# Where a mixer's streamed operands lie against its weights: the distance changed to 36 words

## The chip, the cores and the metric

The kernel runs on one core of a Trainium2 chip. The metric is the device time of one execution in microseconds; the kernel before takes 826.99 us (median of three runs, 826.88 to 827.64). TensorE (PE) multiplies. Each of its matrix products has two operands in SBUF: 128x128 *weights*, which a separate weight load (PEld) brings into the array, and a *moving* operand of up to 512 words for each partition, which is streamed past them. VectorE is DVE, ScalarE is ACT, GpSimd is POOL, SyncE is SP.

## What is computed

One encoder layer on 512 tokens of width 1024, in float32:

```python
x = x + 0.5 * swiglu(rms_norm(x, ffn1_norm), ffn1_w_gate, ffn1_w_up, ffn1_w_down)   # width 2752
h = rms_norm(x, mix_norm)
u = h @ w_in                       # 512 Fourier columns | q 8x64 | k 2x64 | v 2x64
f_out = fourier_mixer(u[..., :512])  # Re(DFT over positions and 128 channels), x4 groups, then a linear map + bias
a_out = gqa_attention(q, k, v)       # head norms, axial rotary, softmax over 512 keys
x = x + concat([f_out, a_out]) @ w_out
x = x + 0.5 * swiglu(rms_norm(x, ffn2_norm), ffn2_w_gate, ffn2_w_up, ffn2_w_down)
y = rms_norm(x, final_norm)
```

## The kernel before

The layer is computed transposed: tiles have features on the partitions and the 512 tokens along them. To keep float32 accuracy, an operand is split in a high part, rounded to the matrix format, and the low rest; a product is then three matrix products (high x high, high x low, low x high), all added in one PSUM bank (`product`, L179). Most 512-word moving operands are read through `turned` (L176), which takes groups of 4 words 16 words apart, 32 of them, and comes back for the next 4 words; the text calls these *strided*, the others *flat*. The results of a bank are moved out by DVE and ACT.

There are three stages. FFN1 (about 0 to 339 us of the profile) and FFN2 (490 to 825) stream gate, up and down weights from HBM by DMA, split them in ACT and DVE, and multiply on PE. Between them lies the mixer. In the mixer the order of all five engines is written out by hand in the string `ORDER`; each of its words is one operation. Its matrix products are:

- projections k, q0 to q3, v: `hh`/`hl` (normed x, high and low) move, weights `w_in` lie in ring slots. (L183)
- Fourier projections f0 to f3 (L1014, L1015, L1016, `fproject_ops`): here pieces of `hh`/`hl` are the weights, and `w_in` moves, flat, 256 words.
- scores (L1150, L1151, `score_ops`): queries in `part` are weights, keys `ks` move, strided.
- transposes of the probabilities `e` (L1176), then values (L1219, `attended_ops`): `vst` is the weights, the transposed probabilities `ph` and `pl` move, strided.
- the transform over positions (L1073, `position_ops`): `eh`/`el` are weights, the tables `pos` move flat, 256 or 258 words, and `both` strided.
- the transform over channels (L185 to L188, called by `channel_ops`): `mapw` is weights, the spectra `dh`, `dl` move, flat, 256 or 258 words.
- results y0 to y7 (L183, `output_ops`): `w_out` lies in ring slots and in `more`, and `part` (mixed output and attention) moves, strided; 8 x 8 x 3 = 192 products.

The change is about addresses, so here is how they come about. SBUF tiles of a pool lie one behind the other, in the order in which they are made. `room(pool, n)` makes an unused tile of n bytes that only shifts what follows. All large tiles have lengths that are multiples of 64 words plus a known rest, so that an operand's place can be told by its address in words modulo 64, and all pieces of an operand share it, save where the text says otherwise. The *distance* of a product is the place of the moving operand less that of the weights, modulo 64. The places before, from the order and sizes of the tiles:

| operand | place | | operand | place |
|---|---|---|---|---|
| ring slots, `more` (weights) | 48 | | `near`: `part`, `eh`, `el`, `vst` | 36 |
| `hh`, `hl`, old spectra in them | 36 | | `ks`, `both`, `ph`, `pl`, `e` | 24 |
| Fourier weights (`FURTHER`) | 20 | | `pos` pieces of 258 words | 24, 26, 28, 30 |
| `chan` | 48 | | `pos` pieces of 256 words | 32 |
| FFN `at` / `rt` | 36 / 32 | | last tokens' weights `tw` (`ASIDE`) | 24 |

So the distance is 52 in the results, scores, values, projections and the FFN's strided products, 48 in the Fourier projections and the FFN's flat ones, 52 to 60 in the position transform, and 0 in the channel transform. In the last 10 us, `by_tokens` (L521, products on L533) uses `at` as weights and `tw` as the moving operand, 384 words, strided: distance 52.

The tiles of the mixer lie where FFN1's `at`, `rt` and `sums` tiles were, and FFN2's lie there after them; the framework makes a tile's first writer wait for the last readers of what was there. FFN2's opening uses four slots of its activation tile as weight slots (`lent`, L554), which fall on mixer tiles that the results still read.

Of the kernel before, what the change touches and what calls it, by code (L numbers as in the profile page):

```python
# [7 lines left out]
F32R = mybir.dt.float32r  # L8
# [5 lines left out]
P = 128  # L14
S = 512
D = 1024
KD = D // P
# [4 lines left out]
HD = 64  # L22
EPS = 1e-6
WARM = 9
FURTHER = 36
FURTHER_IN = "f0", "f1", "f2", "f3"
ROOM = 64
FRONT, LOWER, NEAR = 16, -12, 4
ASIDE = 40
NS = 12  # L30

GROUPS1 = ((0, "t", 1, 2), range(3, 9), range(9, 15), range(15, 21))
# [53 lines left out]
def encoder(ctx, tc, A, out):  # L86
# [4 lines left out]
    whole = cp.tile([P, FRONT + NS * KD * P + 2 * ROOM], F32R, name="ring")  # L91
# [3 lines left out]
    def room(pool, n):  # L95


        pool.tile([P, n // 4], F32, name=f"room{len(rooms)}")
        rooms.append(n)
# [6 lines left out]
    def bank(name):  # L106
# [7 lines left out]
    hh, hl = (  # L114
        [whole[:, k * KD * P + o * S + NEAR : k * KD * P + (o + 1) * S + NEAR] for k in range(KD)] for o in range(2)
    )
# [9 lines left out]
    def lows(lo, src, hi):  # L126
        nc.vector.tensor_tensor(out=lo, in0=src, in1=asf(hi), op=ALU.subtract)  # L127
# [7 lines left out]
    def further(tile, i, rooms=0):  # L135
        o = i * KD * P + rooms * ROOM + FURTHER
        return tuple(tile[:, o + j * KD * P : o + (j + 1) * KD * P].rearrange("p (a b) -> p a b", b=P) for j in range(2))
# [38 lines left out]
    def turned(ap):  # L176
        return ap.rearrange("p (a b c) -> p b a c", b=4, c=4)

    def product(ps, whi, wlo, mhi, mlo, first, last, cut=False, turn=False):  # L179
        if turn:  # L180
            ps, mhi, mlo = turned(ps), turned(mhi), turned(mlo)
            for a, b in ((whi, mhi), (whi, mlo), (wlo, mhi)):
                nc.tensor.matmul(ps, a, b, start=first and b is mhi and a is whi, stop=last and a is wlo)  # L183
            return
        nc.tensor.matmul(ps, whi, mhi, start=first, stop=False)  # L185
        for t in parts_of(CUT[0]) if cut else (slice(0, ps.shape[-1]),):
            nc.tensor.matmul(ps[:, t], whi, mlo[:, t], start=False, stop=False)
        nc.tensor.matmul(ps, wlo, mhi, start=False, stop=last)  # L188
# [92 lines left out]
    def ffn(norm, after, wgu, wd, wdt, groups, opening, closing):  # L281
# [6 lines left out]
        with tc.tile_pool(name=f"act{n_}", bufs=1) as ap, tc.tile_pool(name=f"sums{n_}", bufs=2) as sp:  # L288
# [7 lines left out]
            def place(j):  # L296
# [5 lines left out]
            tw = [  # L302
                ring[:, 3 * i * KD * P + ASIDE : 3 * i * KD * P + ASIDE + PLACES * LAST * P]
                .rearrange("p (m c) -> p m c", c=LAST * P) for i in range(2)
# [441 lines left out]
    n2 = Norm(2)  # L746
    with tc.tile_pool(name="mix", bufs=1) as mp, tc.tile_pool(name="mixt", bufs=1) as mt:

        room(mp, 96)
        kst = [[mp.tile([P, S], F32R, name=f"ks{v}{o}") for o in range(2)] for v in range(2)]  # L750
        both = mp.tile([P, S], F32R, name="both")
        pos = mp.tile([P, 4 * 258 + 3 * 256], F32R, name="pos")
        near = mp.tile([P, 18 * S + 2 * NEAR], F32R, name="near")
        part = [near[:, NEAR + i * S : NEAR + (i + 1) * S] for i in range(16)]
        eh, el = ([[part[4 * n + 2 * h + i].rearrange("p (a b) -> p a b", a=2) for i in range(2)] for h in range(2)] for n in range(2))
        vst = near[:, NEAR + 16 * S : NEAR + 18 * S].rearrange("p (v c o e) -> p v c o e", v=2, c=4, o=2)
        room(mp, 32)
        more_tile = mp.tile([P, 2 * KD * P + ROOM], F32R, name="more")
        more = [slot_at(more_tile, i) for i in range(2)]
        plain.extend(more)  # L760
# [5 lines left out]
        sin = mp.tile([P, S], F32, name="sin")  # L766
        chan = mp.tile([P, 4, P], F32R, name="chan")

        coss = [[pos[:, (2 * p + i) * 258 : (2 * p + i + 1) * 258] for i in range(2)] for p in range(2)]
        sins = [[None, pos[:, 1032:1288]], [pos[:, 1288:1544], pos[:, 1544:1800]]]  # L770
        sc = mp.tile([P, 4, 10], F32, name="sc")


        ops = {}

        def op(name):
            def put(f):
                assert name not in ops, name
                ops[name] = f
                return f  # L780

            return put
# [4 lines left out]
        def bank_for(name, readers=1):  # L787
            held[name] = [spare.pop(0), readers]
            return held[name][0]

        def read(name):
            held[name][1] -= 1
            if not held[name][1]:
                spare.append(held.pop(name)[0])
# [248 lines left out]

        mh, ml = ([e[g // 2][g % 2].rearrange("p a b -> p (a b)") for g in range(4)] for e in (eh, el))
        mapw = [(hh[0], hl[0]), (hh[1], hl[1])]

        def fold_ops(t):


            @op(f"map{t}")  # L1050
            def _():
                banks[f"map{t}"] = bank_for(f"map{t}")
                whi, wlo = (w[:, :4, :].rearrange("p a b -> p (a b)") for w in ws["fw"])
                product(banks[f"map{t}"], chan[:, 2 * t, :], chan[:, 2 * t + 1, :], whi, wlo, True, True)

            op(f"map{t}.h")(lambda: nc.scalar.copy(mapw[t][0], banks[f"map{t}"]))

            @op(f"map{t}.l")
            def _():
                lows(mapw[t][1], banks[f"map{t}"], mapw[t][0])  # L1060
                read(f"map{t}")

        def position_ops(g):


            gs = slice(g % 2 * P, (g % 2 + 1) * P)
            dh, dl = hh[2 + g % 2], hl[2 + g % 2]
            name = f"d{g}"

            def add(w, m, t, order=lambda ps: ps):  # L1070
                ps, first = banks[name], not started
                started.append(t)
                nc.tensor.matmul(  # L1073
                    order(ps[:, t]), w, m, start=first, stop=len(started) == 12, skip_group_check=True
                )

            started = []

            def sums(o):
                if not started:  # L1080
                    banks[name] = bank_for(name, 1)
                for i in range(2):
                    h, l = (e[g // 2][i][:, o, gs] for e in (eh, el))
                    t, m = (slice(256, 512), sins) if o else (slice(0, 258), coss)
                    if o and i == 0:
                        add(h, turned(both), slice(0, S), turned)
                        add(l, turned(both), slice(0, S), turned)
                    else:
                        add(h, m[0][i], t)
                        add(l, m[0][i], t)  # L1090
                    add(h, m[1][i], t)

            op(f"{name}0")(lambda: sums(0))
            op(f"{name}1")(lambda: sums(1))
            op(f"{name}.h")(lambda: nc.scalar.copy(dh, banks[name]))

            @op(f"{name}.l")
            def _():
                lows(dl, banks[name], dh)
                read(name)  # L1100
# [2 lines left out]

        def channel_ops(g):
            gs = slice(g * P, (g + 1) * P)
            dh, dl = hh[2 + g % 2], hl[2 + g % 2]

            @op(f"c{g}.c")
            def _():
                banks[f"pc{g}"] = pc = bank_for(f"pc{g}")  # L1110
                product(pc[:, 0:258], mapw[0][0][:, gs], mapw[0][1][:, gs], dh[:, 0:258], dl[:, 0:258], True, True)

            @op(f"c{g}.s")
            def _():
                banks[f"ps{g}"] = psn = bank_for(f"ps{g}")
                product(psn[:, 0:256], mapw[1][0][:, gs], mapw[1][1][:, gs], dh[:, 256:512], dl[:, 256:512], True, True)

            @op(f"c{g}.q")
            def _():
                fos[g, 0] = mt.tile([P, 256], F32, tag="fq", name=f"fq{g}")  # L1120
                nc.scalar.copy(fos[g, 0], banks[f"ps{g}"][:, 0:256])
                read(f"ps{g}")

            @op(f"c{g}.o")
            def _():
                q, pc = fos[g, 0], banks[f"pc{g}"]
                fos[g, 1] = o = tp.tile([P, S], F32, tag="g", name=f"fo{g}")
                b = fb[:, g : g + 1]
                nc.vector.tensor_scalar(
                    out=o[:, 0:257:256], in0=pc[:, 0:257:256], scalar1=b, scalar2=None, op0=ALU.add  # L1130
                )
                for out, how in ((o[:, 1:256], ALU.add), (o[:, 257:512], ALU.subtract)):
                    nc.vector.scalar_tensor_tensor(out=out, in0=pc[:, 1:256], scalar=b, in1=q[:, 1:256], op0=ALU.add, op1=how)
                read(f"pc{g}")

            op(f"c{g}.h")(lambda: nc.scalar.copy(mh[g], fos[g, 1]))
            op(f"c{g}.l")(lambda: lows(ml[g], fos[g, 1], mh[g]))
# [429 lines left out]
```

## Time and profile before

| | us |
|---|---|
| median of three runs | 826.99 |
| the profiled execution, its own time | 827.06 |
| its span, first to last instruction | 824.8 |
| PE busy / weight load busy | 816.9 / 750.4 |
| DVE / ACT busy | 639.2 / 464.6 |

What lies outside the span is 827.06 - 824.8 = 2.26 us. A PE product's record includes its way through the array, so records of neighbours overlap: a product is longer in the record than the step from its start to the next one's. Where products follow each other, the pace is the length of a row of them divided by their count.

### The profile page before, as it was taken

To read this page: it belongs to the slowest core of one execution; us is meant where nothing else is said; L and a number is where in the kernel's file an instruction comes from. 1 tells how busy PE (TensorE), PEld (TensorE's weight loads), DVE (VectorE), ACT (ScalarE), POOL (GpSimd) and SP (SyncE) were. 2 spreads that over 40 slices of the span, in tenths; PEclk is the share of its full clock that TensorE was granted. 3 is DMA by queue.
4 is the path that set the end of the run, shared out by engine and by line. 5 is a ranking of instruction groups with operands and counts; after the bars stand their busy time and mean duration, and the time that the engine had idled before them with its cause. 6 is when DMAs were issued, how large, how long until landed. Compare 5 with 4: busy or idle time off the path is not lost.

```text
span 824.8 us, 13679 instructions
## 1 busy us (share of the span) xinstructions
PE 816.9 (99%) x5406; PEld 750.4 (91%) x5406; DVE 639.2 (78%) x1005; ACT 464.6 (56%) x778; POOL 30.7 (4%) x34
## 2 busy tenths in 40 slices
PE   9999999999999999999999999999999999999997
PEld 7889999899989998888999888899988999899986
DVE  7998896489756947699998488998955896479574
ACT  7764664167524645677786357556632674256462
POOL 0110000000000000221100000100000000000001
PEclk9999999999999999999999999999999999999999
DMA  7664322323242213522020224453232332422222
GB/s 256 180 145 173 122 91 77 122 103 141 78 140 102 64 55 115 184 93 77 26 77 27 82 97 116 119 163 123 90 122 94 128 116 63 138 103 97 69 77 103
DMA packets 31168, 89.58 MB, mean 109 GB/s; under 512 B 3712, under 2 KB 8832, under 8 KB 31104
## 3 DMA queue, kind: packets, MB, share of 16 engines
q1 hardware_dynamic: 27776, 82.61, 29.2%
q0 software_dynamic: 2608, 5.12, 3.4%
q8 instruction: 42, 0.69, 0.3%
q10 hardware_dynamic: 720, 0.98, 0.3%
q14 instruction: 22, 0.18, 0.1%
HBM read 84.24 MB, written 2.10 MB: 105 GB/s over the span
## 4 chain that ended last, share of the span: by engine, by line
PE 92%; DVE 5%; issue 1%; ACT 0%; DMA 0%; POOLq 0%; POOL 0%; DVEq 0%; ACTq 0%
PE dn L183 25%; PE r L419 23%; PE q L419 12%; PE gu L183 8%; PE mix L183 7%; PE p L419 6%; PE gu L708 3%; PE mix L1219 1%; PE mix L1176 1%; DVE mx L1156 1%; PE mix L1073 1%; DVE pl L127 1%; PE mix L1015 1%; PE mix L1016 1%; PE mix L1014 1%
## 5 line engine op out<-in xcount | busy, mean ns | idle before, releaser
L419 PE MATMUL r<-rt,ring 128*128 128x256 f32 x1686 | 209.2, 276 | 0.0
L183 PE MATMUL dn<-at,ring 128*128 128x512 f32 x900 | 203.3, 381 | 0.5 <-DVE ring L127 0.4
L419 PEld LDWEIGHTS r<-rt,ring 128*128 128x128 f32 x1686 | 200.3, 188 | 0.8
L183 PEld LDWEIGHTS dn<-at,ring 128*128 128x128 f32 x900 | 168.0, 188 | 29.8 <-DVE ring L127 1.6
L419 PE MATMUL q<-rt,ring 128*128 128x256 f32 x840 | 106.6, 276 | 0.0
L127 DVE TENSOR_TENSOR ring<-s,ring 128x1024 fp32r<-128x1024 f32 x70 | 85.4, 1220 | 24.1 <-ACT ring L378 20.8
L419 PEld LDWEIGHTS q<-rt,ring 128*128 128x128 f32 x840 | 100.4, 188 | 0.0
L543 DVE SCALAR_TENSOR_TENSOR gx<-dn,gx 128x512 f32<-128x512 f32 x61 | 41.9, 688 | 67.6 <-PE dn L183 67.6
L378 ACT CAST ring<-s 128x1024 fp32r<-128x1024 f32 x70 | 73.5, 1050 | 28.0 <-PE p L419 13.7
L169 ACT CAST ring<-raw_dn 128x768 fp32r<-128x768 f32 (+3 forms) x58 | 45.2, 783 | 71.3 <-PE dn L183 62.1
L127 DVE TENSOR_TENSOR ring<-raw_dn,ring 128x768 fp32r<-128x768 f32 (+3 forms) x58 | 51.5, 891 | 5.6 <-PE r L419 4.4
L419 PE MATMUL p<-rt,ring 128*128 128x256 f32 x420 | 53.3, 276 | 0.0
L127 DVE TENSOR_TENSOR ring<-raw_g,ring 128x1024 fp32r<-128x1024 f32 x35 | 42.7, 1219 | 11.1 <-PE p L419 10.2
L419 PEld LDWEIGHTS p<-rt,ring 128*128 128x128 f32 x420 | 50.2, 188 | 0.0
L183 PE MATMUL gu<-ring 128*128 128x512 f32 x216 | 48.9, 381 | 0.0
L183 PEld LDWEIGHTS gu<-ring 128*128 128x128 f32 x216 | 40.4, 188 | 6.9
L378 ACT CAST ring<-raw_g 128x1024 fp32r<-128x1024 f32 x35 | 36.8, 1051 | 16.0 <-DMA raw_g<-in_wgu 8.8
L427 ACT COPY p<-r 128x256 f32<-128x256 f32 x35 | 12.9, 370 | 46.7 <-PE r L419 46.3
L451 ACT ACTIVATE g<-g 128x512 f32<-128x512 f32 x35 | 22.2, 633 | 23.4 <-DVE g L450 23.1
L387 ACT CAST ring<-raw_u 128x512 fp32r<-128x512 f32 x35 | 21.8, 624 | 16.6 <-PE q L419 16.0
L255 POOL TENSOR_TENSOR r<-ms,mhalf 128x4 f32<-128x4 f32 (+1 forms) x4 | 4.3, 1072 | 659.5 <-DVE ms L248 659.5
L464 DVE TENSOR_TENSOR u<-g,u 128x512 f32<-128x512 f32 x35 | 24.0, 685 | 6.1 <-ACT u L463 6.0
(271 smaller groups left out, 1323.1 us busy)
## 6 DMA issues: line engine op xcount, KB each, us to landing
raw_g<-in_wgu SPq DMA_DIRECT2D x35, 512.0 KB, 3.6
raw_u<-in_wgu SPq DMA_DIRECT2D x35, 512.0 KB, 4.3
raw_dn<-in_wd SPq DMA_DIRECT2D x40, 384.0 KB, 3.1
raw_gu<-in_wgu SPq DMA_DIRECT2D x12, 512.0 KB, 3.5
raw_o<-in_wo SPq DMA_DIRECT2D x8, 512.0 KB, 3.5
raw_dn<-in_wd SPq DMA_DIRECT2D x8, 448.0 KB, 3.4
raw_wq<-in_wins SPq DMA_DIRECT2D x4, 512.0 KB, 5.1
raw_f<-in_winf SPq DMA_DIRECT2D x4, 512.0 KB, 4.1
```

Of the source, the lines that this page charges most:

```text
L127: nc.vector.tensor_tensor(out=lo, in0=src, in1=asf(hi), op=ALU.subtract)
L169: nc.scalar.copy(hi[:, :n, :], raw[:, :n, :])
L183: nc.tensor.matmul(ps, a, b, start=first and b is mhi and a is whi, stop=last and a is wlo)
L378: nc.scalar.copy(hi, src)
L387: nc.scalar.copy(hi, src)
L419: nc.tensor.matmul(ps[:, t], a[:, ks], b[:, i, t], start=first and i == 0 and o == 0, stop=i == KH - 1 and o == 2, skip_group_check=not first,
L427: nc.scalar.copy(t, ps)
L451: nc.scalar.activation(b["g"], b["g"], AF.Silu)
L464: nc.vector.tensor_tensor(out=u, in0=b["g"], in1=u, op=ALU.mult)
L543: nc.vector.scalar_tensor_tensor(out=x[d][:, t], in0=ps[:, t], scalar=0.5, in1=x[d][:, t], op0=ALU.mult, op1=ALU.add)
L708: nc.tensor.matmul(turned(pss[c]), w[:, k % 2, c], turned(m[k]), start=k == 0 and m is hh and w is hi, stop=k == KD - 1 and w is lo,)
L1014: nc.tensor.matmul(ps, hh[k][:, cs], whi[:, a, :], start=k == 0, stop=False)
```

## The change

Six sets of places move; the number, order and shapes of the instructions stay. `near` becomes the first large tile of the mixer's pool and starts at place 20 (`STEP` = 4 words after its base at 16). `more`, `cos`, `sin` and `chan` follow, `more` and `chan` again at place 48. Then 32 bytes of room put `ks`, `both` and `pos` on place 56; a last room puts the pool of `e`, `ph` and `pl` on place 56 too, 128 bytes further than before. `FURTHER` = 24 puts the moving Fourier weights on place 8, `ASIDE` = 24 does so for the last tokens' weights, and `spectra` is a new set of views of the ring tile, 36 words behind the old ones, on place 8. The distances become 36 in results, scores, values, Fourier projections, channel transform and `by_tokens`; 36, 38, 40, 42 and 44 for `pos`, 36 for `both`. Projections and the FFN's other products keep theirs, and so does the product of `chan` with the linear map (distance 0, flat, 512 words). The new spectra reach 36 words into `hl[2]`, `hh[3]`, `hl[3]` and `hh[4]`.

```diff
-FURTHER = 36
+FURTHER = 24
...
-FRONT, LOWER, NEAR = 16, -12, 4
-ASIDE = 40
+FRONT, LOWER, NEAR, STEP = 16, -12, 4, 4
+ASIDE, ASIDE_D = 24, 36
...
+        room(mp, 64)
+        near = mp.tile([P, 18 * S + 2 * STEP], F32R, name="near")
+        part = [near[:, STEP + i * S : STEP + (i + 1) * S] for i in range(16)]
...
+        vst = near[:, STEP + 16 * S : STEP + 18 * S].rearrange("p (v c o e) -> p v c o e", v=2, c=4, o=2)
         room(mp, 96)
+        more_tile = mp.tile([P, 2 * KD * P + ROOM], F32R, name="more")
...
+        cos = mp.tile([P, S], F32, name="cos")
+        sin = mp.tile([P, S], F32, name="sin")
+        chan = mp.tile([P, 4, P], F32R, name="chan")
+
+        room(mp, 32)
         kst = [[mp.tile([P, S], F32R, name=f"ks{v}{o}") for o in range(2)] for v in range(2)]
         both = mp.tile([P, S], F32R, name="both")
         pos = mp.tile([P, 4 * 258 + 3 * 256], F32R, name="pos")
-        near = mp.tile([P, 18 * S + 2 * NEAR], F32R, name="near")
...
-        room(mp, 32)
-        more_tile = mp.tile([P, 2 * KD * P + ROOM], F32R, name="more")
...
         sc = mp.tile([P, 4, 10], F32, name="sc")
+        room(mp, 64)
...
+        spectra = [
+            [whole[:, o : o + S] for o in ((2 + i) * KD * P + j * S + NEAR + ASIDE_D for j in range(2))] for i in range(2)
+        ]
...
-            dh, dl = hh[2 + g % 2], hl[2 + g % 2]
+            dh, dl = spectra[g % 2]
```

The last replacement stands in `position_ops` and in `channel_ops`.

More of the change, by code (lines that the diff above doesn't have):

```diff
@@ L747, in encoder @@
     with tc.tile_pool(name="mix", bufs=1) as mp, tc.tile_pool(name="mixt", bufs=1) as mt:
-        room(mp, 96)
-        kst = [[mp.tile([P, S], F32R, name=f"ks{v}{o}") for o in range(2)] for v in range(2)]
-        both = mp.tile([P, S], F32R, name="both")
-        pos = mp.tile([P, 4 * 258 + 3 * 256], F32R, name="pos")
-        near = mp.tile([P, 18 * S + 2 * NEAR], F32R, name="near")
-        part = [near[:, NEAR + i * S : NEAR + (i + 1) * S] for i in range(16)]
-        eh, el = ([[part[4 * n + 2 * h + i].rearrange("p (a b) -> p a b", a=2) for i in range(2)] for h in range(2)] for n in range(2))
-        vst = near[:, NEAR + 16 * S : NEAR + 18 * S].rearrange("p (v c o e) -> p v c o e", v=2, c=4, o=2)
-        room(mp, 32)
+        room(mp, 64)
+        near = mp.tile([P, 18 * S + 2 * STEP], F32R, name="near")
+        part = [near[:, STEP + i * S : STEP + (i + 1) * S] for i in range(16)]
+        eh, el = ([[part[4 * n + 2 * h + i].rearrange("p (a b) -> p a b", a=2) for i in range(2)] for h in range(2)] for n in range(2))
+        vst = near[:, STEP + 16 * S : STEP + 18 * S].rearrange("p (v c o e) -> p v c o e", v=2, c=4, o=2)
+        room(mp, 96)
         more_tile = mp.tile([P, 2 * KD * P + ROOM], F32R, name="more")
@@ L767, in encoder @@
         chan = mp.tile([P, 4, P], F32R, name="chan")
+        room(mp, 32)
+        kst = [[mp.tile([P, S], F32R, name=f"ks{v}{o}") for o in range(2)] for v in range(2)]
+        both = mp.tile([P, S], F32R, name="both")
+        pos = mp.tile([P, 4 * 258 + 3 * 256], F32R, name="pos")
         coss = [[pos[:, (2 * p + i) * 258 : (2 * p + i + 1) * 258] for i in range(2)] for p in range(2)]
@@ L1105, in channel_ops @@
             gs = slice(g * P, (g + 1) * P)
-            dh, dl = hh[2 + g % 2], hl[2 + g % 2]
+            dh, dl = spectra[g % 2]
             @op(f"c{g}.c")
```

## The prediction

> **What bounds the kernel now.** First the page: its opening, and the shares of the chain of work that ended last.
>
> ```profile
> span 824.8 us, 13679 instructions
> PE 816.9 (99%) x5406; PEld 750.4 (91%) x5406; DVE 639.2 (78%) x1005; ACT 464.6 (56%) x778; POOL 30.7 (4%) x34
> PE 92%; DVE 5%; issue 1%; ACT 0%; DMA 0%; POOLq 0%; POOL 0%; DVEq 0%; ACTq 0%
> ```
>
> PE is the bound, and a change of its pace is a change of the time, wherever the chain runs over PE. Next, the stretches of the mixer (busy times of PE, PEld, DVE, ACT, POOL, counts in brackets), and pieces of the chain there and in FFN2 (start, length, what).
>
> ```profile
> 350.00:393.00 43.00, 42.72 (x260) 37.65 (x259) 41.36 (x86) 32.81 (x65) 8.43 (x5) 1.00 0.27 86
> 393.00:450.00 57.00, 57.00 (x403) 52.73 (x402) 53.50 (x108) 43.57 (x90) 2.46 (x4) 1.00 0.13 47
> 450.00:490.00 40.00, 40.00 (x183) 34.10 (x182) 24.31 (x33) 16.64 (x25) 0.00 (x0) 1.00 0.23 79
> ```
>
> ```profile
> 385.58 0.62 DVE pl L127
> 387.44 0.69 DVE pl L127
> 389.53 0.61 DVE mx L1156
> 393.26 0.12 PE mix L1016
> 449.72 40.30 PE mix L183 x183
> 579.45 2.72 PE r L419 x24
> ```
>
> Until about 393 us the chain runs over DVE (maxima, low parts); from there PE is busy in 57.00 of 57.00 and 40.00 of 40.00 us, at a granted clock of 1.00. So the price of each distance counts from 393 on, and at the very end. The last two rows give the pace of an undisturbed stream: results 40.30 / 183 = 220.2 ns at distance 52, FFN2's flat products 2.72 / 24 = 113.3 ns at 48.
>
> Third, whether a distance costs anything now. Groups by form, before the bar the count, behind it busy time and mean record in ns:
>
> ```profile
> L419 PE MATMUL r<-rt,ring 128*128 128x256 f32 x1674 | 209.0, 276 | 0.0
> L183 PE MATMUL mix<-near,ring 128*128 128x512 f32 x120 | 28.1, 381 | 0.0
> L1015 PE MATMUL mix<-ring 128*128 128x256 f32 x48 | 13.3, 277 | 0.0
> L1016 PE MATMUL mix<-ring 128*128 128x256 f32 x48 | 13.3, 277 | 0.0
> L1151 PE MATMUL mix<-ks,near 128*128 128x512 f32 x32 | 12.3, 385 | 0.0
> L1219 PE MATMUL mix<-pl,near 128*128 128x512 f32 x32 | 12.2, 383 | 0.0
> L1073 PE MATMUL mix<-pos,near 128*128 128x256 f32 x16 | 2.5, 280 | 0.0
> L1073 PE MATMUL mix<-both,near 128*128 128x512 f32 x8 | 2.5, 388 | 0.0
> L188 PE MATMUL mix<-ring 128*128 128x258 f32 x4 | 1.1, 284 | 0.0
> L187 PE MATMUL mix<-ring 128*128 128x256 f32 x4 | 1.1, 280 | 0.0
> L187 PE MATMUL mix<-ring,chan 128*128 128x512 f32 x2 | 0.8, 394 | 0.0
> ```
>
> ```profile
> L1014 PE MATMUL mix<-ring x48: 275/275/367, 374.8 to 425.8; 128*128 128x256 f32 x48
> L1073 PE MATMUL mix<-pos,near x40: 275/282/369, 429.8 to 444.2; 128*128 128x258 f32 x24, 128*128 128x256 f32 x16
> L1219 PE MATMUL mix<-ph,near x32: 380/384/493, 373.8 to 448.0; 128*128 128x512 f32 x32
> L533 PE MATMUL last<-ring,at x42: 325/328/419, 809.6 to 818.3; 128*128 128x384 f32 x42
> ```
>
> (The second fence has least, median and longest record; in these groups pauses spoil the mean.) The floor of a record is 275 ns for a flat product of 256 words and 380 for a strided one of 512. The FFN and the results sit on it. The mixer's short stretches lie 2 to 8 ns above, and the product of `chan` with the linear map, at distance 0, is 14 ns above the strided floor. So a place does cost, though single nanoseconds.
>
> The Trainium skill says otherwise. On its page "TensorE: Matmul & The Clock Gate", Part 2, PE has two independent read ports of SBUF, and loading the next weights takes no read bandwidth from the running matmul; by that, the change is worth 0 and the time stays at 827.0. The rows disagree: 280 to 284 ns beside 276 for nearly the same length.
>
> **Which pair matters.** The timeline shows when weights are loaded:
>
> ```profile
> 484.37 5.25 PEld L183 LDWEIGHTS mix<-near,ring 128*128 128x128 f32 x24
> 484.59 5.44 PE L183 MATMUL mix<-near,ring 128*128 128x512 f32 x24
> 426.35 0.38 PE L1151 MATMUL mix<-ks,near 128*128 128x512 f32 x1
> 426.57 0.39 PE L185 MATMUL mix<-ring,chan 128*128 128x512 f32 x1
> 426.80 0.40 PE L187 MATMUL mix<-ring,chan 128*128 128x512 f32 x1
> 427.03 0.40 PE L188 MATMUL mix<-ring,chan 128*128 128x512 f32 x1
> ```
>
> The loads begin 0.22 us ahead of their products, which is one product. So what streams beside a moving operand is the *next* product's weights. In the third row keys (place 24) stream while `chan` (48) is loaded: distance 40, the nearest to 36 that a strided product has here, and the step to the next start is 0.22 us, the floor. The next two steps, at distance 0, are 0.23. I take 36 for strided streams as clean, like 40.
>
> For flat streams the nearest row is a single one. The Fourier product at 393.26 in the chain (place 20) ends its group and streams while the weights of a transpose (place 48) are loaded: distance 36, and its step is 0.12 us where undisturbed ones are 0.113. One sample, with weights of another kind; it is a warning, and one end of the range.
>
> **The change part by part.** It adds and removes no instruction, DMA or queue entry; it moves places. Counts from 393 us on (busy, count in brackets: L1014, L1151, L1219, L1073):
>
> ```profile
> 393.00:450.00 57.00, 12.48 (x45) 1.00 0.13 47
> 393.00:450.00 57.00, 5.76 (x15) 1.00 0.13 47
> 393.00:450.00 57.00, 13.45 (x48) 1.00 0.13 47
> 393.00:450.00 57.00, 7.64 (x48) 1.00 0.13 47
> ```
>
> What stands above the floor there, and so the most that can be won with the floor as it is:
>
> - Fourier projections, 3 x 45 = 135 products: 277 - 275 = 2 ns each, 0.27 us. Most of their records are on the floor (L1014's median is 275). 48 to 36: I take half, 0.13; ends +0.54 (135 x 4, all like the `pos` and channel rows at 6 above) and -0.27.
> - Scores, 2 x 15 = 30, by L1151's 385 - 380 = 5: 0.15 us. Values, 48, by 384 and 383: 3.5 ns, 0.17 us. But a score or a value is often followed by a transpose, whose weights `e` move to place 56 together with `ks`, `ph` and `pl`: that pair stays at distance 0. I take a quarter of 0.32, 0.08.
> - Position transform: 24 products of 258 words at 282 against some 276, 0.14; 16 at 280, 0.08; 8 strided at 388, 0.06. From 52 to 60 to 36 to 44: half of 0.28, 0.14.
> - Channel transform, 8 x 3 = 24 products, 280 to 284: 6 ns, 0.14 us. It leaves distance 0, the worst place that the rows show; two thirds, 0.09.
> - Results, 192 products: 0.2 ns above 220, nothing to win at the floor.
> - Last tokens, 42 products: median 328 against the least, 325; at most 0.13, taken as 0.
> - Scores, values and Fourier products ahead of 393: hidden by DVE, taken as 0. Were PE the path there too, the same prices on 34, 16 and 57 products would give 34 x 5 + 16 x 3.5 + 57 x 2 = 0.34 us.
>
> Sum 0.13 + 0.08 + 0.14 + 0.09 = 0.44 us, of at most 0.27 + 0.32 + 0.28 + 0.14 + 0.13 = 1.14.
>
> Two more steps are costed at nothing. The waits on reused places: FFN2's borrowed slots fall on later pieces of `part` than before, which the last steps of y7 read. The work that hides this is a copy in front of them:
>
> ```profile
> 489.85 1.05 ACT L169 CAST ring<-raw_gu 128x1024 fp32r<-128x1024 f32 x1 [2.47 <-PE mix L183]
> 490.80 1.04 ACT L169 CAST at<-raw_gu 128x1024 fp32r<-128x1024 f32 x1
> 502.11 5.44 PE L183 MATMUL gu<-ring,at 128*128 128x512 f32 x24
> ```
>
> ACT already waits for the end of the results at 489.85 for a ring slot, writes the borrowed slot (`at`) at 490.80, and the products that need it begin at 502.11; a microsecond of waiting would vanish in 10. The same two rows show a copy to two different places taking 1.05 and 1.04, so I give the moved tiles no price on ACT and DVE. The spectra's 36 words in `hl[2]`, `hh[3]`, `hl[3]` and `hh[4]` add readers and writers in the order of `ORDER`: the Fourier products that read them are issued before d00, and y3.h and y4.h, which write them again, come after c3. No new wait.
>
> The profiled execution's own time is 827.06, 0.07 above the median of 826.99: 827.06 - 0.44 = 826.6, and the same by the median to the tenth.
>
> **The rivals.**
>
> *The new distance collides, and the kernel is slower.* Place: the results above all, the one long stretch that is on the floor now and can only lose. If 36 is to strided streams what distance 0 is in the `chan` row, each pays 14 ns: 30 + 48 + 8 + 192 = 278 products, 3.9 us, less the 0.3 that scores, values and `both` pay already; the 42 last ones three quarters of it, 0.4; the Fourier products 0.5. Together 4.5: 831.6. It decides from 1.65 us (0.2%, about what a measurement of this kernel tells from no change), which is 5.3 ns on some 310 strided products: a pace of the results of 225.5. For it speaks that 36 appears nowhere in this trace but in the 0.12 us row; against it, the 0.22 us at distance 40.
>
> *The floor itself falls.* From 256 to 512 words the pace grows by 220.2 - 113.3 = 106.9 ns, so 220.2 - 2 x 106.9 = 6.4 ns of each product are not spent on words. If half of it is a collision that 52 and 48 merely leave small, 278 + 42 + 135 + 24 + 40 = 519 products win 3.2 ns, 1.7 us, and the 1.14 above as well: 824.2; with all 6.4 ns it would be 822.6. Against it: distances 40, 48 and 52 all end on the same floor, and so do flat and strided streams. The same page of the Trainium skill, under "Back-to-back issue gap", gives N / 2.4 + 2.5 ns for matmuls in a row, 215.8 for 512 words; an estimate by it would be 4.4 ns less per result and 0.8 us over 192. The 220.2 measured is above it.
>
> *Nothing happens.* A stream that is interrupted needs a few products to settle whatever the places are, as the Fourier group does at the distance at which FFN2 runs on the floor. Time 827.0.
>
> **How the numbers follow.** Small gain as summed, 826 to 827: 0.43. Nothing: 0.17. Collision: 0.26, of which 0.22 above 0.2%. Lower floor: 0.14. So faster by over 0.2%: 0.14, within: 0.43 + 0.17 + 0.04 = 0.64, slower: 0.22. The time is that of the first, 826.6, whose own range is 825.8 to 827.4. The range of 8 in 10 reaches to the middle of the lower floor, 824.2, and to two thirds of the collision, 830.0.
>
> **What would show it.** Right: results still at 220 ns in the chain, L187 and L188 in the channel transform near 276, `pos` nearer 276 than 282, Fourier means at 275 to 276, scores and values hardly changed. Wrong: a results piece longer than 40.30 for 183 products (collision), or shorter than 40.2 (lower floor), or a PE row with a DVE or ACT releaser after 393 us that is not there now.

## The result and the profile after

The changed kernel takes 828.34 us (median of 22 runs), the kernel before 826.98 beside it on the same chip: a ratio of 1.0015, 95% interval 1.0008 to 1.0022. It is slower, by 1.36 us; 826.6 was forecast. The profiled execution took 828.41, against 827.06 before, so its 1.35 us more can be followed through the trace. First the page's opening, then pieces of the chain (start, length, what).

```profile
span 826.1 us, 13679 instructions
PE 819.1 (99%) x5406; PEld 751.4 (91%) x5406; DVE 639.0 (77%) x1005; ACT 464.4 (56%) x778; POOL 30.7 (4%) x34
```

```profile
339.89 4.09 PE mix L183 x18
394.01 0.90 PE mix L1224 x4
450.67 40.70 PE mix L183 x183
```

The first two answer to these of the kernel before:

```profile
339.76 4.09 PE mix L183 x18
393.82 0.89 PE mix L1219 x4
```

PE has 2.2 us more of busy time and the weight load 1.0, DVE, ACT and POOL none. The mixer begins 0.13 us later, ahead of anything that the change touches (the opening of FFN1, whose length varies from run to run, see below). The value products that began at 393.82 begin at 394.01: beside the 0.13, less than 0.1 us is lost ahead of them. The results begin at 450.67 in place of 449.72: another 0.76 us are gone between 394 and 450. The results take 40.70 in place of 40.30 us for the same 183 products, 222.4 ns each in place of 220.2: 0.40 us. At the end of the results 0.95 + 0.40 = 1.35 us are lost, as much as in the whole execution; 0.13 of it is the opening's, so some 1.2 us are the change's.

Ahead of 394 us, the slower products are hidden because PE had time to spare behind DVE. In the changed kernel that spare time is used up earlier: from this piece on the chain runs over PE, where before it went back to DVE (378.62 to 379.36 on PE, then a maximum on DVE) and came to PE for good at 391.27.

```profile
378.76 0.49 PE mix L1155
```

Groups by form say which products it was (busy us, mean record in ns; L1016 to L1018 are the Fourier lines that were L1014 to L1016, L1224 the values, L1156 the scores, L1078 the position transform):

```profile
L183 PE MATMUL mix<-near,ring 128*128 128x512 f32 x120 | 28.3, 383 | 0.0
L183 PE MATMUL mix<-near,more 128*128 128x512 f32 x72 | 17.3, 383 | 0.0
L1016 PE MATMUL mix<-ring 128*128 128x256 f32 x48 | 13.7, 285 | 0.0
L1017 PE MATMUL mix<-ring 128*128 128x256 f32 x48 | 13.6, 284 | 0.0
L1018 PE MATMUL mix<-ring 128*128 128x256 f32 x48 | 13.6, 283 | 0.0
L1156 PE MATMUL mix<-ks,near 128*128 128x512 f32 x32 | 12.3, 385 | 0.0
L1224 PE MATMUL mix<-pl,near 128*128 128x512 f32 x32 | 12.2, 383 | 0.0
L533 PE MATMUL last<-ring,at 128*128 128x384 f32 x42 | 8.3, 340 | 0.0
L1078 PE MATMUL mix<-pos,near 128*128 128x256 f32 x16 | 2.5, 280 | 0.0
L1078 PE MATMUL mix<-both,near 128*128 128x512 f32 x8 | 2.4, 386 | 0.0
L187 PE MATMUL mix<-ring 128*128 128x258 f32 x4 | 1.1, 286 | 0.0
L187 PE MATMUL mix<-ring 128*128 128x256 f32 x4 | 1.1, 282 | 0.0
```

The three Fourier lines went from 281, 277 and 277 ns to 285, 284 and 283. The results went from 381 and 380 to 383, which is the 0.40. Scores, values, position and channel transform are where they were, within 4 ns. The median record of the second Fourier line (L1015 before, L1017 now) shows that it is not a few slow products: it was 275, the floor, and is 283.

```profile
L1015 PE MATMUL mix<-ring x48: 275/275/283, 374.9 to 425.9; 128*128 128x256 f32 x48
L1017 PE MATMUL mix<-ring x48: 277/283/289, 375.0 to 426.8; 128*128 128x256 f32 x48
```

What a product costs the path is not its record but the step from its start to the next one's. Added up in both traces, from the value products at 393.82 (394.01) on to the end of the results' 183, the steps show where the time went (all other products of this stretch change by 0.02 us together):

| products | forecast, us | change of their steps, us |
|---|---|---|
| Fourier, 132 | -0.13 | +0.59 (4.5 ns each) |
| scores and values, 78 | -0.08 | +0.15 |
| position and channel transforms, 72 | -0.23 | +0.02 |
| results, 183 | 0 | +0.39 |

So at 36 neither stream settles on its floor. What had to be found out: is it the distance, or the moved tiles; does the place of the moving operand alone do it; and which distances settle.

### The profile page after: what moved, and what is told of

It reads as the page before. It is cut to its first block, busy times and chain, and to the rows that moved or that the text cites. A ratio compares the mean times of both kernels' runs of the same rounds, so it can differ in the third digit from the quotient of the medians.

```text
span 826.1 us, 13679 instructions
## 1 busy us (share of the span) xinstructions
PE 819.1 (99%) x5406; PEld 751.4 (91%) x5406; DVE 639.0 (77%) x1005; ACT 464.4 (56%) x778; POOL 30.7 (4%) x34
## 4 chain that ended last, share of the span: by engine, by line
PE 93%; DVE 4%; issue 1%; DMA 1%; ACT 0%; POOLq 0%; POOL 0%; DVEq 0%; ACTq 0%
PE dn L183 25%; PE r L419 23%; PE q L419 12%; PE gu L183 7%; PE mix L183 7%; PE p L419 6%; PE gu L708 3%; PE mix L1224 2%; PE mix L1181 1%; PE mix L1017 1%; PE mix L1016 1%; PE mix L1018 1%; PE mix L1078 1%; DVE mx L1161 1%; PE mix L1155 1%
```

## The experiments

Theory D: the distance decides whether a stream of products settles on its floor. Rival L: the time is lost by the moved tiles and their neighbours, in no pair of places. Rival P: the place of the moving operand decides, not its distance.

Where a kernel is given without a ratio, its single time is not compared: the opening of FFN1 takes a varying time (18.20 us for its first 80 products in the changed kernel's profile, 19.80 in that of s3, before anything of the change runs). This is mostly no wait: the first products themselves are slower for a while. In s3 the median record of the products that start ahead of 9 us is 628 ns, in the kernel before it is 380. Groups and chain pieces are compared instead. For timed kernels the ratio to the kernel before on the same chip is given.

### Fourier alone (e1)

```diff
--- before
-FURTHER = 36
+FURTHER = 24
```

> The kernel before with the moving Fourier weights alone put 36 words from hh (FURTHER = 24); all other places as before. Theory D (the distance decides whether a stream of products settles on its floor, and 36 lets neither flat nor strided streams settle): L1014 to L1016 go from 277 to 283-285 ns as in the changed kernel, 135 products from 393 us on at 5 to 6 ns, so 0.7 to 0.8 us slower: 827.7 to 827.8; the results stay at 220.2 ns. Rival L (the moved tiles and their neighbours, not the pairs of places, cost the time): 827.0 and 277 ns. Rival P (the place of the moving operand itself, 8 in place of 20, decides): like D in this run.

Measured: 828.26 us beside 827.53, ratio 1.0009 (1.0000 to 1.0018), so 0.7 us. Groups and chain:

```profile
L1014 PE MATMUL mix<-ring 128*128 128x256 f32 x48 | 13.7, 286 | 0.0
L1015 PE MATMUL mix<-ring 128*128 128x256 f32 x48 | 13.6, 283 | 0.0
L1016 PE MATMUL mix<-ring 128*128 128x256 f32 x48 | 13.6, 284 | 0.0
450.65 40.30 PE mix L183 x183
```

One constant gives the whole Fourier loss, and the results begin at 450.65, as in the changed kernel, but stay at 40.30. By steps, the 132 Fourier products behind the first values cost 4.7 ns more each than before, 0.63 us; scores and values, whose places are the old ones here, cost 0.14 more, so that part does not come from their own places. Rival L does not hold for this part.

### All but Fourier (e2)

```diff
--- changed kernel
-FURTHER = 24
+FURTHER = 36
```

> The changed kernel with the moving Fourier weights alone put back to distance 48 (FURTHER = 36). Theory D: L1016 to L1018 return to 277 ns, the results stay at 222.4 ns; 0.7 to 0.8 us faster than the changed kernel, 827.5, still 0.5 above the kernel before. Rival L: 828.3, no gain. Rival P: as D.

Measured: 827.93 us beside 827.53, ratio 1.0008 (0.9999 to 1.0017). Relative to the kernel before, 0.4 us is left of the 1.36 by the medians, 0.7 by the ratio. Groups and chain:

```profile
L1016 PE MATMUL mix<-ring 128*128 128x256 f32 x48 | 13.5, 281 | 0.0
L1017 PE MATMUL mix<-ring 128*128 128x256 f32 x48 | 13.3, 277 | 0.0
L1018 PE MATMUL mix<-ring 128*128 128x256 f32 x48 | 13.3, 277 | 0.0
452.49 40.70 PE mix L183 x183
```

The Fourier groups are back at the means of before, the results stay at 40.70. By the medians the two halves, 0.7 and 0.4, add up to most of 1.36. The timed ratios alone would not separate them from noise; the groups do. (The late start of the results in this profile is the opening's, whose first 80 products took 20.17 us.)

### Distance or place (e3)

Here `hh` and `hl` move, and the Fourier operands that stream past them stay on place 20.

```diff
--- before
-FRONT, LOWER, NEAR = 16, -12, 4
+FRONT, LOWER, NEAR, HERE = 16, -12, 4, 16
...
-        [whole[:, k * KD * P + o * S + NEAR : k * KD * P + (o + 1) * S + NEAR] for k in range(KD)] for o in range(2)
+        [whole[:, k * KD * P + o * S + HERE : k * KD * P + (o + 1) * S + HERE] for k in range(KD)] for o in range(2)
```

> The kernel before with hh and hl on place 48 in place of 36. The moving Fourier weights stay on place 20, but their distance becomes 36 because their weights moved. Theory D: L1014 to L1016 at 283 to 285 ns as in the changed kernel. Rival P (the place of the moving operand decides): 277 ns, as place 20 is kept. Beside it: all strided products that stream hh or hl (gates, tails, projections, some 530) get distance 0; if that costs 14 ns each as in the one flat row of distance 0, the time is some 7 us longer, 834; if strided streams do not mind distance 0, 827.

Measured groups and chain:

```profile
L183 PE MATMUL gu<-ring 128*128 128x512 f32 x216 | 49.9, 386 | 0.0
L1014 PE MATMUL mix<-ring 128*128 128x256 f32 x48 | 13.6, 283 | 0.0
L1015 PE MATMUL mix<-ring 128*128 128x256 f32 x48 | 13.4, 280 | 0.0
L1016 PE MATMUL mix<-ring 128*128 128x256 f32 x48 | 13.4, 280 | 0.0
451.94 40.31 PE mix L183 x183
```

At distance 36 with the old place of the moving operand, the second and third Fourier line take 280 ns (277 at 48, 283 to 284 at 36 in the changed kernel). By steps, the 132 products cost 3.3 ns more each than before, against 4.5 in the changed kernel. Rival P, 277, is out, and so is the place of the weights alone, which e1 did not move; but D's 283 to 285 was not reached either, so the places themselves have some part beside the distance, and that part stays open. The gates now stream at distance 0 and pay 386 - 381 = 5 ns, not the 14 that I had carried over from the flat row at distance 0.

### Both undone (d1)

```diff
--- changed kernel
-FURTHER = 24
+FURTHER = 36
...
-FRONT, LOWER, NEAR, STEP = 16, -12, 4, 4
+FRONT, LOWER, NEAR, STEP = 16, -12, 4, 36
...
-        room(mp, 64)
-        near = mp.tile([P, 18 * S + 2 * STEP], F32R, name="near")
+        near = mp.tile([P, 18 * S + 40], F32R, name="near")
...
-        room(mp, 96)
+        room(mp, 32)
...
-        room(mp, 32)
+        room(mp, 96)
...
-        room(mp, 64)
```

> The changed kernel with both suspects undone: the Fourier products at 48 and, by near on place 36, the results at 52; scores and position transform stay at 36 and more, the channel transform and the last tokens at 36; the values fall to distance 20. Theory D: L1016 to L1018 at 277 ns, results 220.2 ns, and what is left of the change is worth 0.1 to 0.3 us: within 0.05% of the kernel before. Rival L (moved tiles cost something that is in no pair of places): still 0.5 to 1 us slower.

Measured: 828.0 us beside 827.37, ratio 1.0004 (0.9995 to 1.0013; the medians are 0.63 us apart, by the ratio it is 0.3); chain and groups:

```profile
L1015 PE MATMUL mix<-ring 128*128 128x256 f32 x48 | 13.3, 277 | 0.0
L1016 PE MATMUL mix<-ring 128*128 128x256 f32 x48 | 13.3, 277 | 0.0
450.08 40.26 PE mix L183 x183
```

With the two distances back, both groups are on their old pace, though all tiles lie as in the changed kernel's order. The results begin 0.36 us later than before: 0.12 of it is lost ahead of the first values, and 0.16 is in the steps of the values, which lie at distance 20 and have 386 ns in their `pl` products against 383. Behind the results the profile loses another 0.3 us in FFN2, which the changed kernel does not, and the cause of that is open. The interval reaches from no loss to 1.1 us, most of the change's, so the time of this run does not decide between D and L; its groups do, for the two that matter.

### Other distances (s1, s2, s3, s4)

Four kernels vary `FURTHER`, the place of `near` (by `STEP` and the rooms around it), `ASIDE` and `ASIDE_D` together; each group has its own distance. The edit shown is that of s1; the figures in its first line are `FURTHER`, `STEP` and `ASIDE` of each kernel.

```diff
--- changed kernel          s1: 4, 24, 28   s2: 20, 32, 8   s3: 40, 4, 20   s4: 28, 40, 36
-FURTHER = 24
+FURTHER = 4
...
-FRONT, LOWER, NEAR, STEP = 16, -12, 4, 4
-ASIDE, ASIDE_D = 24, 36
+FRONT, LOWER, NEAR, STEP = 16, -12, 4, 24
+ASIDE, ASIDE_D = 28, 48
...
-        room(mp, 64)
-        near = mp.tile([P, 18 * S + 2 * STEP], F32R, name="near")
+        near = mp.tile([P, 18 * S + 24], F32R, name="near")
```

> The changed kernel with other distances: Fourier 16 (flat), results 40 and last tokens 40 (strided), channel transform 48, scores and values 32, position transform 32 to 40. Theory D with the place in lines of 16 words (flat streams settle where the distance is a multiple of 16, as 48 is): Fourier at 275 to 277 ns. Theory D with every distance of its own: no forecast for 16. For strided streams the five steps seen at 40 forecast 220.2 ns for the results and 328 for the last tokens. Rival P gives no forecast for new places; that settled and unsettled values do not go with the distances would speak for it.

> Distances: Fourier 32 (flat), results 48 (strided), last tokens 20 (strided), channel transform 16, scores and values 24. Theory D with lines of 16 words for flat streams: 32 settles like 48 and 16, L1015 to L1017 at 277 to 278 ns after the first. For strided streams only 52 has settled so far: results at 222 to 226 ns.

> Distances: Fourier 52 (flat), results 20 (strided, 52 less 32), last tokens 32, channel transform 32, scores and values 52. Theory D with lines of 16 words: flat 52 is 4 off a multiple of 16, as 36 is: 283 to 285 ns. If strided streams repeat every 32 words, results at 20 take 220.2 ns as at 52; if they repeat every 64 words only, 222 to 226.

> Distances: Fourier 40 (flat), results 56 (strided, 4 words beside 52), last tokens 48, channel transform 52, scores and values 16. Theory D with lines of 16 words: flat 40 lies midway between multiples of 16: 281 to 285 ns. Results at 56: 220.2 if what settles is a range around 52, 222 to 226 if it is 52 alone.

The results' chain pieces, in the order s1, s2, s3, s4, and after them one Fourier line (the second of the three) of each:

```profile
450.27 41.40 PE mix L183 x183
```

```profile
453.06 41.47 PE mix L183 x183
```

```profile
452.63 42.06 PE mix L183 x183
```

```profile
450.69 41.48 PE mix L183 x183
```

```profile
L1016 PE MATMUL mix<-ring 128*128 128x256 f32 x48 | 13.3, 278 | 0.0
```

```profile
L1016 PE MATMUL mix<-ring 128*128 128x256 f32 x48 | 13.6, 283 | 0.0
```

```profile
L1016 PE MATMUL mix<-ring 128*128 128x256 f32 x48 | 13.6, 282 | 0.0
```

```profile
L1016 PE MATMUL mix<-ring 128*128 128x256 f32 x48 | 13.4, 280 | 0.0
```

Divided by 183 and put beside the others:

| results, strided: distance | 52 | 36 | 40 | 48 | 56 | 20 |
|---|---|---|---|---|---|---|
| us for 183 | 40.30 | 40.70 | 41.40 | 41.47 | 41.48 | 42.06 |
| ns each | 220.2 | 222.4 | 226.2 | 226.6 | 226.7 | 229.8 |

| Fourier, flat: distance | 48 | 16 | 40 | 52 | 32 | 36 |
|---|---|---|---|---|---|---|
| ns, second line's mean | 277 | 278 | 280 | 282 | 283 | 284 |

For strided streams 52 stands alone among the six; four words beside it, at 48 and 56, the product costs 6.4 and 6.5 ns more, and it does not repeat after 32 words (20 is the worst). 36 is the second best of those tried. For flat streams 48 and 16 settle and 32 does not, which refutes the rule of multiples of 16 that I had put into the expectations of s1 to s4; 16 and 48 fit a period of 32 words, and two points are no proof of it. (16 is not quite like 48: in s1 some groups stay on 276 ns, others alternate between 278 and 281 to their end.)

Two limits of these rows. Within each of them only the moving operand's place varies, with the weights on 48 in the results and on 36 in the Fourier products, so they do not tell distance from place; for flat streams e1 and e3 do, in part, and for strided ones no run here does. And the order of the results' row does not carry over to short groups: in s2 the last tokens stream at distance 20, the worst of the row, and their mean of 339 ns lies between the 338 of the kernel before and the 341 of e3, both at distance 52:

```profile
L533 PE MATMUL last<-ring,at 128*128 128x384 f32 x42 | 8.3, 339 | 0.0
```

Of the distances tried, those of the kernel before are the best for both streams, so nothing points to a version that beats both kernels.

## Why the prediction was wrong

**What bounds the kernel, and where a pace counts:** right in the main. PE carries the path from 393 us on, and the loss by the end of the results (1.35 us, 0.13 of it the opening's) is that of the time (1.36); what the Fourier products lose ahead of 393 is hidden but for less than 0.1 us. But the spare time that hides it is not fixed: in the changed kernel the chain is on PE from 378.76.

**"I take 36 for strided streams as clean, like 40":** wrong, and this is the step that failed for the results. The row it rested on is one product in a short stretch. In a row of 183, distance 40 costs 226.2 ns (s1), and still 13 of those 183 steps are 220 ns in the trace. A single step on the floor does not show that a stream stays there. The term "nothing to win at the floor" was 0.40 us of loss.

**The Fourier term, "48 to 36: I take half, 0.13":** wrong in sign, and the largest error: +0.59 us by steps. The one flat row at distance 36, the 0.12 us step at 393.26, pointed the right way; I called it a warning and took the other side. But it could not have decided: in the trace it is 120 ns, and so is a step of the same group at distance 48, the one from L1015 at 392.12. That it pointed the right way was luck. The end that I had named, +0.54 (4 ns more on 135 products), was close: 4.5 ns on 132.

**The gains in the position and channel transforms, 0.14 and 0.09:** not there. L1078 stays at 280 for 256 words, and L187 goes to 282 and 286 from 280 and 282 (256 and 258 words). s1 puts the channel transform at 48, the best flat distance, and its lines L187 and L188 still take 280 to 282, among them:

```profile
L188 PE MATMUL mix<-ring 128*128 128x258 f32 x4 | 1.1, 282 | 0.0
L188 PE MATMUL mix<-ring 128*128 128x256 f32 x4 | 1.1, 281 | 0.0
```

Three products in a row lie above the floor at each of the distances tried (0, 36, 48). This fits the remark in "Nothing happens" that an interrupted stream needs a few products to settle, and the Fourier groups of the kernel before show such settling: record by record, up to nine products at the start of a group take 277 to 283 ns, and almost all others 275. For the channel transform itself it is argued, not shown by a run of its own.

**Scores and values "hardly changed":** right for the records, 385 and 383 as before; in their steps the gain of 0.08 that the sum had was a loss of 0.15. **Waits on reused places at nothing:** right; PE gets no new pause (its idle time ahead of the scores is 0.3 us before and 0.1 after), and the loss is in the pace of the streams.

**The rivals.** What happened is the collision, given 0.26, with its place right in part and its price wrong for the strided products: the results pay 2.2 ns, not 14, and less than the 5.3 from which it was to decide. The flat Fourier products, which it priced at 0.5 us, pay 0.59, more than the results. Gates at distance 0 in e3 show that 14 was too much for strided streams even there: 5. The lower floor did not appear at any distance tried. The two independent read ports of the Trainium skill's page "TensorE: Matmul & The Clock Gate", Part 2, would make all distances equal; 220.2 to 229.8 ns for one shape and order of products does not agree with it.

## What to carry to other kernels

Where PE is the bound, the places of the two operands that are read at the same time are worth some nanoseconds per product, and the best distance depends on the reading pattern: take it from a long stream of the same pattern, never from a single step or from the other pattern. Short stretches of three to twelve products hardly got better at any distance here, so look for such a gain first where products run in long rows. (One did: the eight `both` products went from 388 to 381 ns in s1, 0.05 us by steps.) When a change puts one number in place of two that were found separately, price each stream that leaves its own number as a loss until a row shows otherwise.

## What was not expected of the hardware

A long stream does not scatter about its mean: at each distance it falls into a pattern of steps that repeats to its end. In the results, start to start in the traces, 176 of the 183 steps at distance 52 are 220 ns. At 20 the steps alternate between 226 and 234, at 56 they are 226, 227, 227, and at 36 a row of nine between 219 and 226 comes back unchanged. At 48 about one step in five is 220: a single step on the floor says nothing. In the Fourier products at 36 the records run through 286, 283, 289, 280, 278 over and over in the longer groups, and never settle on 275.

The cost is not smooth in the distance: strided, 52 words cost 220.2 ns and 48 or 56 cost 226.6 and 226.7. Distance 0 is not the worst for a strided stream (5 ns a product in e3, against 9.6 at 20 in s3). And the same distance of 36 costs the flat Fourier products 280 ns at one pair of places (20 and 48) and 283 to 284 at another (8 and 36); why is open.
